# Twelve weight granules multiplied as plain float32, and fewer weight subtractions on GpSimd, in a chain of two transformer blocks

## The chip, the cores and the metric

The kernel runs on one core of one Trainium2 chip, as one program. The metric is the time of one execution in microseconds (us) on the device; the number to be forecast is the median of the runs. All data are float32.

## What is computed

Two blocks follow each other on 256 tokens of 2048 features. `w_o`, `w_up`, `cc_in` and `cc_out` below are the weights of the four products that the change touches (`cc_in` and `cc_out` are `w_in` and `w_out` of `conformer_conv`).

```python
# first block
mod = c_act @ w_ada + b_ada                    # six vectors: sh1, sc1, gt1, sh2, sc2, gt2
h = rmsnorm(x, g_mix) * (1 + sc1) + sh1
x = x + (1 + gt1) * mixer(h, ...)              # ends with  merged @ w_o
h = rmsnorm(x, g_ffn) * (1 + sc2) + sh2
u = h @ w_up                                   # 2048 -> 11264
x = x + (1 + gt2) * ((silu(a) * b) @ w_down)   # a, b: u after three taps along tokens
x = rmsnorm(x, g_final)
# second block
h = rmsnorm_2(x, norm1_g)
# conformer_conv(h, ...):
u = h @ w_in + b_in                            # cc_in, 2048 -> 4096
u = val * sigmoid(gate)
u = causal_dwconv(u, dw) + dw_b                # 31 taps along tokens
u = silu(layernorm(u, ln_g, ln_b))
x = x + u @ w_out + b_out                      # cc_out, 2048 -> 2048
x = x + square(relu(rmsnorm_2(x, norm2_g) @ w1)) @ w2
x = rmsnorm_2(x, final_g)
```

## The kernel before

**Granules.** Every weight matrix is cut into granules of 128 x 1024 floats (512 KB). SyncE issues their transfers in the order of use (`issue`, L191) into a ring of six buffers named `raw`. TensorE multiplies float32r numbers, which keep less of a float than float32; so each granule is split into two parts: ScalarE copies it to float32r (`hi`, `split_hi`, L196, four buffers), and VectorE or GpSimd subtracts that copy from the raw granule (`lo`, `split_lo`, L204, three buffers). The operand is split the same way, two feature tiles at a time, into a tile `xs` (eight buffers). TensorE then sums three products per tile (`products`, L252): hi with the operand's hi, hi with its lo, lo with its hi. A granule is two row tiles of four output tiles, so it makes 2 x 4 x 3 = 24 matmuls of 128 x 256. Eight granules fill a group of four output tiles over all 2048 input features; the products here consist of such groups (`gemm`, L277), four for `w_o` and `cc_out`, 22 for `w_up`, seven for `cc_in` and two of half the width for `cc_last`, which is the rest of the same matrix.

**Order.** The program is written as a list of items, one a granule, and emitted item by item; each engine works through its own instructions in that order. When item i's matmuls are emitted, `hi` is emitted up to item i + 3, and operand preparation and `lo` up to item i + 2 (`split_to`, LA = 2). A raw buffer is free again when its `lo` is done, two granules ahead of the matmuls. Some items carry a granule of `w_ada` as an extra: a dot product on VectorE (L374), placed by `fill_ada`; the first 74 units of the last three tiles of the modulation (`IN_MIX`) lie among the items of `w_in`, the remaining 22 among those of `w_o`.

**Which engine subtracts.** The table `GPSIMD` names the granules whose `lo` GpSimd makes: `w_o` 0 to 7, `w_up` 10 to 17, `cc_in` from 8 on and `cc_last`, `cc_out` 0 to 7 (and every third granule of another stretch). VectorE makes all others.

**Operands at the four places.** In the first group of `w_o` the operand pairs come from the merged gates `mg`, which VectorE is still finishing (L868, L875, L876), by `o_prep`: a copy on ScalarE (L226) and a subtraction on VectorE (L227). The first groups of `w_up` and `cc_in` take x without the norm's factor r, which isn't known yet (`early_up`, `early_prep`, through `split_scaled`, L273 and L274); their sums are scaled afterwards. r is computed while granule 4 of that group is emitted (`norm2`, `norm3`). The second groups take the normed operand: `h_prep` for `w_up` (VectorE L581, ScalarE L582, VectorE L588) and `g_prep` for `cc_in` (VectorE L603, ScalarE L604, VectorE L608), pair by pair. In `cc_in` VectorE also runs the 31 taps, with the running sum in PSUM (L1178, L1181). `cc_out` waits behind a barrier (`ln`): the layer norm's mean and factor come from TensorE (L390), then `s_first` subtracts the mean and multiplies by the factor on VectorE into one of two pair tiles (L1349, L1350), ScalarE applies silu (L1353) and copies (L1354), and `s_second` subtracts (L1358); `rescale` of x (L1118) lies between.

Of the kernel before, what the change touches and what calls it, by code (L numbers as in the profile page):

```python
# [18 lines left out]
P = 128  # L19
# [18 lines left out]
# columns of the packed per-feature vectors, in the two parts they are loaded in  # L38
# [20 lines left out]
# columns of the constants  # L59
# [33 lines left out]
class Item:  # L93
    """One granule of matrix products: half a unit of weights, and what goes with it."""

    def __init__(self, uses, mm=None):
        self.uses, self.mm = uses, mm
        self.pool = False
        self.prep = self.post = self.barrier = self.also = self.enter = None
        self.extra = []  # L100
# [3 lines left out]
def block_kernel(ctx: ExitStack, tc: tile.TileContext, t):  # L104
# [3 lines left out]
    GPSIMD = {"w_up": (10, 18), "w_o": (0, 8), "cc_in": (8, 54), "cc_last": (0, 8), "cc_out": (0, 8)}  # L108
    SIDE = 4
    P13, S14, P14, S15, P15 = 8, 10, 12, 8, 14  # L110
    IN_MIX = 74
# [36 lines left out]
    def second_vectors():  # L148
        """What the feed-forwards need takes the place of the activated condition."""
# [28 lines left out]
    items = []  # L178
    epi = deque()
# [18 lines left out]
    def split_lo(it):  # L198
        it.lo = wp.tile([P, 1024], FR, tag="lo", name="lo")
        w, k = it.uses  # L200
        # VectorE is busy with the operands of a first group, and with the convolution
# [5 lines left out]
    class Pairs:  # L207
        """Operands as pairs of feature tiles, each split into two float32r parts."""
# [15 lines left out]
    def split_x(dst, src):  # L224
        """dst: [P, 2, 2, S] float32r; src: [P, 2, S]."""
        nc.scalar.activation(dst[:, 0], src, AF.Copy)  # L226
        nc.vector.tensor_tensor(dst[:, 1], src, dst[:, 0].bitcast(F32), op=OP.subtract)  # L227

    def products(it, ps, xs, k0, kpg, nk, G, tok):
        """The products of one granule; the operand of the first row tile starts the sums."""  # L230
# [23 lines left out]

    def outputs(ps, G, tok, cols=S):
# [4 lines left out]
    def finish_epis(seq):  # L260
        """The epilogues of groups up to that number."""
# [7 lines left out]
    def split_scaled(dst, p, scale):  # L269
        """A pair of tiles of x, each times its column."""  # L270
# [6 lines left out]
    def gemm(w, g, nk, xs, epis, G=4, prep=None, tok=False, barrier=None, post=None, hook=None,  # L277
             whole=False):
        """One group of G output tiles: nk row tiles of the weights in granules of 1024 columns."""
# [5 lines left out]
        def mm(it, k0):  # L285
# [5 lines left out]
            products(it, st["ps"], xs, k0, kpg, nk, G, tok)  # L291
# [8 lines left out]
        for gi in range(ng):  # L300
            it = Item((w, g * ng + gi), lambda it, k0=gi * kpg: mm(it, k0))
            if prep:
                it.prep = lambda k0=gi * kpg: prep(k0 // 2)
# [6 lines left out]
    def lead(w, sets, chunks, xs, prep, feed):  # L310
        """Sets of four groups that take turns in all banks, by chunks of pairs of row tiles; between
        its turns a group's sums wait where its results will go."""
# [55 lines left out]
    def ada(n, half):  # L368
        """Half of the products of one tile of the modulation."""
# [8 lines left out]
    def ada_sum(a, b):  # L378
        """The modulation's tiles a to b of six."""
# [5 lines left out]

    def spread(cols, name):
        """[tokens, 2] to [P, S], the same in every partition."""
# [14 lines left out]
    class Stat:  # L402
        """Sums of squares over the features of tiles that come one by one, and with a gain those
        of the scaled features too: the early tiles' are added up first, the late ones go straight
        to the tensor engine, as [tokens, block * count + which]."""
# [51 lines left out]
    def rope(dst, ps, which, then=None):  # L457
        """dst = ps * cos + swapped halves * signed sin."""
# [13 lines left out]

    def start():
# [20 lines left out]
        # the first norm's sums, between the products of the first rows' modulation  # L494
# [29 lines left out]
    def angles():  # L524
        """The angles of both tables, reduced to -pi..pi."""
# [13 lines left out]
    def tables(w):  # L539
        """Cosine and signed sine from the reduced angle."""  # L540
# [9 lines left out]
    def piped(first, second, n):  # L550
        """A step of preparation that starts the next pair before it ends its own."""
# [16 lines left out]
    def h_prep(A, B, ready=None):  # L568
        """Pairs of (x * rstd) * A + B."""
# [22 lines left out]
    def g_prep(A):  # L592
        """Pairs of x * A * rstd."""
# [1044 lines left out]
```

## Time and profile before

| what | value |
|---|---|
| runs, us | 2649.13, 2643.74, 2645.97 (median 2645.97) |
| profiled execution, span from first to last instruction | 2641.8 us |
| profiled execution, time of its own as a run | not stated; its span is 1.9 us below the fastest run and 4.2 us below the median |
| mean granted TensorE clock | 0.993 |
| TensorE busy | 2568.7 us, 97% of the span |
| VectorE busy | 1884.2 us, 71% |
| ScalarE busy | 1414.5 us, 54% |
| GpSimd busy | 306.8 us, 12% |
| `hi` on ScalarE | 858 granules, mean 1061 ns |
| `lo` on VectorE | 771 granules, mean 1229 ns |
| `lo` on GpSimd | 87 granules, mean 2485 ns |

A profile lists, for each engine, groups of instructions by source line with the idle time just before them and the instruction that ended it. An engine that is idle and is not the one that sets the end costs nothing. The granted clock is the share of TensorE's full speed: 1.00 is its upper level of 2.4 GHz, 0.50 its lower level of 1.2 GHz. One matmul of two float32r tiles is one row of the trace; one of plain float32 is two.

### The profile page before, as it was taken

To read this page: it belongs to the slowest core of one execution; us is meant where nothing else is said; L and a number is where in the kernel's file an instruction comes from. 1 tells how busy PE (TensorE), PEld (TensorE's weight loads), DVE (VectorE), ACT (ScalarE), POOL (GpSimd) and SP (SyncE) were. 2 spreads that over 40 slices of the span, in tenths; PEclk is the share of its full clock that TensorE was granted. 3 is DMA by queue.
4 is the path that set the end of the run, shared out by engine and by line. 5 is a ranking of instruction groups with operands and counts; after the bars stand their busy time and mean duration, and the time that the engine had idled before them with its cause. 6 is when DMAs were issued, how large, how long until landed. Compare 5 with 4: busy or idle time off the path is not lost.

```text
span 2641.8 us, 51155 instructions
## 1 busy us (share of the span) xinstructions
PE 2568.7 (97%) x20774; PEld 2520.1 (95%) x20774; DVE 1884.2 (71%) x2742; ACT 1414.5 (54%) x2039; POOL 306.8 (12%) x206
## 2 busy tenths in 40 slices
PE   6999999999899999999999998998999999999998
PEld 5899999999898999999999998998999999999998
DVE  6887877868879666677677679987644444666765
ACT  5776664445346444444565555655544444555553
POOL 1201200000303000000000018983000000000000
PEclk9999999999999999999999999999999999999999
DMA  9998767778784777676555554434555555555553
GB/s 320 321 333 316 246 222 240 252 242 281 242 298 162 229 225 223 224 224 224 190 184 185 185 180 143 163 128 141 174 188 184 184 186 186 180 184 185 186 184 125
DMA packets 153599, 559.35 MB, mean 212 GB/s; under 512 B 17041, under 2 KB 17425, under 8 KB 153361
## 3 DMA queue, kind: packets, MB, share of 16 engines
q1 hardware_dynamic: 153362, 556.08, 62.9%
q8 instruction: 162, 2.65, 0.4%
q14 instruction: 75, 0.61, 0.1%
HBM read 553.91 MB, written 2.10 MB: 210 GB/s over the span
## 4 chain that ended last, share of the span: by engine, by line
PE 56%; issue 32%; DVE 8%; DMA 1%; ACT 1%; POOL 1%; DVEq 0%; POOLq 0%; SPq 0%; ACTq 0%
PE g L252 50%; PE v L252 3%; DVE lo L204 1%; DVE raw L374 1%; DMA raw<-in_w_ada 1%; DVE dc L1181 1%; PE ln L1225 0%; DVE xs L608 0%; DVE vec L603 0%; DMA raw<-in_w_in 0%; DVE hn L581 0%; POOL side L1168 0%; DVE xs L588 0%; DVE xs L227 0%; DVE xs L1358 0%
## 5 line engine op out<-in xcount | busy, mean ns | idle before, releaser
L252 PE MATMUL g<-xs,hi 128*128 128x256 f32 x12640 | 2283.0, 283 | 26.7 <-DVE xs L588 6.4
L252 PEld LDWEIGHTS g<-xs,hi 128*128 128x128 f32 x12640 | 1957.7, 190 | 36.6 <-DVE xs L608 7.3
L252 PE MATMUL g<-xs,lo 128*128 128x256 f32 x6320 | 1785.6, 283 | 5.1 <-DVE lo L204 5.1
L196 ACT ACTIVATE hi<-raw 128x1024 fp32r<-128x1024 f32 x858 | 910.1, 1061 | 1029.5 <-PE g L252 590.9
L204 DVE TENSOR_TENSOR lo<-raw,hi 128x1024 fp32r<-128x1024 f32 x771 | 946.8, 1229 | 436.1 <-PE g L252 237.6
L252 PEld LDWEIGHTS g<-xs,lo 128*128 128x128 f32 x6320 | 1200.3, 190 | 6.2 <-DVE lo L204 6.1
L204 POOL TENSOR_TENSOR lo<-raw,hi 128x1024 fp32r<-128x1024 f32 x87 | 215.8, 2485 | 558.6 <-PE g L252 417.0
L374 DVE SCALAR_TENSOR_TENSOR raw<-raw,crow 128x1024 f32<-128x1024 f32 x192 | 242.8, 1267 | 13.9 <-DMA raw<-in_w_ada 13.4
L227 DVE TENSOR_TENSOR xs<-hid,xs 128x512 fp32r<-128x512 f32 x128 | 88.7, 693 | 120.0 <-ACT xs L226 119.7
L1181 DVE SCALAR_TENSOR_TENSOR dc<-gu,vec,dc 128x256 f32<-128x256 f32 x372 | 148.6, 483 | 0.2
L227 DVE TENSOR_TENSOR xs<-f,xs 128x512 fp32r<-128x512 f32 x88 | 61.0, 693 | 76.1 <-ACT xs L226 75.9
L399 POOL TENSOR_TENSOR small<-small,mh 128x2 f32<-128x2 f32 x3 | 2.9, 979 | 927.7 <-DVE small L398 927.7
L252 PE MATMUL v<-xs,hi 128*128 128x256 f32 x512 | 92.0, 281 | 0.0
L1083 POOL TENSOR_TENSOR small<-small,mh 128x2 f32<-128x2 f32 x1 | 0.7, 693 | 722.2 <-DVE small L1084 722.2
L252 PEld LDWEIGHTS v<-xs,hi 128*128 128x128 f32 x512 | 79.0, 189 | 0.0
L226 ACT ACTIVATE xs<-hid 128x512 fp32r<-128x512 f32 x128 | 78.6, 615 | 0.0
L252 PE MATMUL v<-xs,lo 128*128 128x256 f32 x256 | 72.5, 283 | 1.3 <-DVE lo L204 1.3
L226 ACT ACTIVATE xs<-f 128x512 fp32r<-128x512 f32 x88 | 54.1, 615 | 0.0
L252 PE MATMUL g<-hi,xs 128*128 128x512 f32 x128 | 43.3, 410 | 9.3 <-ACT xs L582 6.8
L252 PEld LDWEIGHTS v<-xs,lo 128*128 128x128 f32 x256 | 48.4, 189 | 1.6 <-DVE lo L204 1.5
L991 ACT ACTIVATE cv<-g,vec 128x256 f32<-128x256 f32 x84 | 45.9, 546 | 0.0
L1168 POOL TENSOR_TENSOR side<-side,tap 128x256 f32<-128x256 f32 x58 | 44.9, 786 | 3.0 <-ACT tap L1165 1.9
(270 smaller groups left out, 1376.9 us busy)
## 6 DMA issues: line engine op xcount, KB each, us to landing
raw<-in_w SPq DMA_DIRECT2D x256, 512.0 KB, 3.4
raw<-in_w_ada SPq DMA_DIRECT2D x192, 512.0 KB, 4.8
raw<-in_w_in SPq DMA_DIRECT2D x176, 512.0 KB, 4.7
raw<-in_w_up SPq DMA_DIRECT2D x176, 512.0 KB, 4.2
raw<-in_w_down SPq DMA_DIRECT2D x88, 512.0 KB, 3.3
raw<-in_cc_in SPq DMA_DIRECT2D x56, 512.0 KB, 3.3
raw<-in_w_o SPq DMA_DIRECT2D x32, 512.0 KB, 4.8
raw<-in_cc_out SPq DMA_DIRECT2D x32, 512.0 KB, 3.3
```

Source lines behind the costliest of these rows:

```text
L196: nc.scalar.activation(it.hi, raws[it.uses], AF.Copy)
L204: eng.tensor_tensor(it.lo, raws[it.uses], it.hi.bitcast(F32), op=OP.subtract)
L226: nc.scalar.activation(dst[:, 0], src, AF.Copy)
L227: nc.vector.tensor_tensor(dst[:, 1], src, dst[:, 0].bitcast(F32), op=OP.subtract)
L252: nc.tensor.matmul(o, l, r, start=(first and n == 0), stop=(last and n == 2), skip_group_check=True)
L374: nc.vector.scalar_tensor_tensor(r, r, 1.0, two["c"][:, half * 1024:(half + 1) * 1024], op0=OP.mult, op1=OP.mult, accum_out=part[:, half, ...
L399: nc.gpsimd.tensor_tensor(v, v, mh, op=OP.pow)
L991: nc.scalar.activation(u, ps, AF.Identity, scale=w[2], bias=vcol("conv_b", j))
L1083: nc.gpsimd.tensor_tensor(r2, r2, mh, op=OP.pow)
L1168: nc.gpsimd.tensor_tensor(sums, sums, x, op=OP.add)
L1181: return lambda: nc.vector.scalar_tensor_tensor(acc["t"], u[:, k:k + S], w(k), acc["t"], op0=OP.mult, op1=OP.add)
```

## The change

The first three granules of the first group of `w_o`, `w_up`, `cc_in` and `cc_out` become plain: 8 float32 matmuls on the raw weights and the unsplit operand, with no `hi`, no `lo` and no `xs`. Their raw buffers are free only when TensorE has read them. The unsplit operand is `mg`, x scaled on ScalarE into a free place (`xv`), and `cu`. `w_o` and `cc_out` need the split pairs 0 to 2 from their second group on: these are made during that group. In the second groups of `w_up` and `cc_in` pair 0 is prepared right after r, and the others earlier than before by up to two granules (`ahead`). GpSimd keeps the `lo` of `cc_in` and `cc_last` alone; 24 others leave it, six of which belong to plain granules, so 18 go to VectorE. In `cc_out` the normed operand is made in place, so the preparation no longer waits for one of two pair tiles. `rescale` starts four items later. Four more granules of `w_ada` move into `w_in`, and none lies in the first four items of `w_o`. The diff also drops comments and docstrings, so line numbers shift (before to after): L204 to L216, L227 to L239, L374 to L403, L581 to L610, L588 to L617, L868 to L897, L1349 to L1400, L1350 to L1401, L1358 to L1411. The plain matmuls are at L275.

```diff
-    GPSIMD = {"w_up": (10, 18), "w_o": (0, 8), "cc_in": (8, 54), "cc_last": (0, 8), "cc_out": (0, 8)}
+    GPSIMD = {"cc_in": (8, 54), "cc_last": (0, 8)}
+    PO, PU, PC, PL = 3, 3, 3, 3
-    IN_MIX = 74
+    IN_MIX = 78
+    def also(n, f):
+        g = items[n].also
+        items[n].also = (lambda: (g(), f())) if g else f
+    def ahead(prep):
+        return lambda p: [prep(q) for q in ((1, 2) if p == 0 else (p + 2,)) if q < KD // 2]
+    def plain_products(it, ps, x, cols, k0, kpg, nk, G):
+        outs = outputs(ps, G, False, cols)
+        w = raws[it.uses]
+        for kk in range(kpg):
+            k = k0 + kk
+            for i in range(G):
+                c = (kk * G + i) * P
+                nc.tensor.matmul(outs[i], w[:, c:c + P], x(k), start=(k == 0 and (i % 2 == 0 or len(ps) == G)),
+                                 stop=(k == nk - 1), skip_group_check=True)
...
-            products(it, st["ps"], xs, k0, kpg, nk, G, tok)
+            if it.plain:
+                plain_products(it, st["ps"], plain, xs.cols, k0, kpg, nk, G)
+                used(it.uses)
+            else:
+                products(it, st["ps"], xs, k0, kpg, nk, G, tok)
...
+            it.plain = plain is not None and gi < {"w_o": PO, "w_up": PU, "cc_in": PC, "cc_out": PL}[w]
...
-    def o_prep(p):
-        split_x(xs_o.new(p), m[f"mg{p // 4}"][:, 2 * (p % 4):2 * (p % 4) + 2])
+    def o_prep(p, late=False):
+        if (p < PO) == late:
+            split_x(xs_o.new(p), m[f"mg{p // 4}"][:, 2 * (p % 4):2 * (p % 4) + 2])
...
-             prep=o_prep if i == 0 else None, hook=o_start if i == 0 else None)
+             prep=(o_prep, lambda p: o_prep(p, True))[i] if i < 2 else None, hook=o_start if i == 0 else None,
+             plain=(lambda k: m[f"mg{k // 8}"][:, k % 8]) if i == 0 else None)
...
-    fill_ada(us[IN_MIX:], n1, len(items) - 4)
+    fill_ada(us[IN_MIX:], n1 + 4, len(items) - 4)
...
+        if p < PU:
+            if p == 0:
+                m["xv"] = slot(7, "xv").rearrange("p a s -> p (a s)")[:, 0:2 * PU * (S + 2)].rearrange(
+                    "p (k s) -> p k s", s=S + 2)
+            for k in (2 * p, 2 * p + 1):
+                nc.scalar.activation(m["xv"][:, k, 0:S], xres[:, k], AF.Copy, scale=aff[:, 2, k:k + 1])
...
+            return
         split_scaled(xs_v.new(p), p, lambda k: aff[:, 2, k:k + 1])
...
-        gemm("w_up", g, KD, xs_u if g else xs_v, es, prep=(early_up, prep_u)[g] if g < 2 else None)
+        gemm("w_up", g, KD, xs_u if g else xs_v, es, prep=(early_up, ahead(prep_u))[g] if g < 2 else None,
+             plain=None if g else lambda k: m["xv"][:, k])
     items[n2 + 4].also = norm2
+    also(n2 + 5, lambda: prep_u(0))
...
+        if p < PC:
+            if p == 0:
+                m["xv"] = slot(6, "xv")
+            for k in (2 * p, 2 * p + 1):
+                nc.scalar.activation(m["xv"][:, k], xres[:, k], AF.Copy, scale=aff[:, 4, k:k + 1])
+            return
         split_scaled(xs_0.new(p), p, lambda k: aff[:, 4, k:k + 1])
...
-             prep=(early_prep, prep_c)[g] if g < 2 else None)
+             prep=(early_prep, ahead(prep_c))[g] if g < 2 else None, plain=None if g else lambda k: m["xv"][:, k])
     items[at_cc + 4].also = norm3
+    also(at_cc + 5, lambda: prep_c(0))
...
+        bg.extend([lambda: None] * 4)
         for j in range(KD):
             bg.append(lambda j=j: rescale(j))
...
     def s_first(p):
-        d = xs_s.new(p)
-        us[p] = u = pair_tile()
-        c = m["u"][p // 4][:, 2 * (p % 4):2 * (p % 4) + 2]
-        nc.vector.tensor_tensor(u, c, wide(stage["mu"]), op=OP.subtract)
+        u = normed(p)
+        nc.vector.tensor_tensor(u, u, wide(stage["mu"]), op=OP.subtract)
         nc.vector.tensor_tensor(u, u, wide(stage["r1"]), op=OP.mult)
...
-        nc.scalar.activation(d[:, 0], u, AF.Copy)
+        if p >= PL:
+            nc.scalar.activation(xs_s.new(p)[:, 0], u, AF.Copy)
...
+    def s_late(p):
+        if p < PL:
+            split_x(xs_s.new(p), normed(p))
...
-             prep=s_prep if i == 0 else None, barrier=ln if i == 0 else None)
+             prep=(s_prep, s_late)[i] if i < 2 else None, barrier=ln if i == 0 else None,
+             plain=(lambda k: m["u"][k // 8][:, k % 8]) if i == 0 else None)
...
-            if items[x].uses:
+            if items[x].uses and not items[x].plain:
                 split_lo(items[x])
...
-                if items[at["hi"]].uses:
+                if items[at["hi"]].uses and not items[at["hi"]].plain:
                     split_hi(items[at["hi"]])
```

Three places where the order of VectorE's instructions is different (rows are line, operation, out<-in, size, and how many in sequence):

VectorE where `w_o` begins; before, `xs<-mg` are the pairs 0 to 2, and the `lo` of their granules are GpSimd's:

```order
L868 TENSOR_TENSOR mg_7374<-g,ga_5122 128x256
L374 SCALAR_TENSOR_TENSOR raw,part<-raw,crow 128x1024
L227 TENSOR_TENSOR xs<-mg_6819,xs 128x2x256
L868 TENSOR_TENSOR mg_7374<-g,ga_5122 128x256
L374 SCALAR_TENSOR_TENSOR raw,part<-raw,crow 128x1024
L227 TENSOR_TENSOR xs<-mg_6819,xs 128x2x256
L868 TENSOR_TENSOR mg_7374<-g,ga_5122 128x256
L374 SCALAR_TENSOR_TENSOR raw,part<-raw,crow 128x1024
L227 TENSOR_TENSOR xs<-mg_6819,xs 128x2x256
```

and in the changed kernel, where the first `xs` is that of pair 3 and a `lo` follows it:

```order
L897 TENSOR_TENSOR mg_7386<-g,ga_5128 128x256
L216 TENSOR_TENSOR lo<-raw,hi 128x1024
L897 TENSOR_TENSOR mg_7386<-g,ga_5128 128x256 x3
L410 TENSOR_TENSOR mod<-part 128x16
L411 TENSOR_TENSOR mod<-mod,vec 128x16
L989 TENSOR_SCALAR aff<-mod 128x16
L904 TENSOR_TENSOR mb<-g,gb_6414 128x256
L239 TENSOR_TENSOR xs<-mg_6831,xs 128x2x256
L216 TENSOR_TENSOR lo<-raw,hi 128x1024
```

Three operand splits and three dot products of `w_ada` are gone from between and behind the last `mg` products; the subtractions of granules 3 to 7 of the group are now on VectorE, one behind each `xs`.

VectorE from the moment when r of `w_up` is there (`hn` is the normed x, `xs<-hn` the operand's lo, `vec<-g` the scaling of the first group's sums); before:

```order
L204 TENSOR_TENSOR lo<-raw,hi 128x1024
L581 SCALAR_TENSOR_TENSOR hn<-xres,aff,r_9141 128x256 x2
L588 SCALAR_TENSOR_TENSOR xs<-hn,mod,xs 128x256 x2
L581 SCALAR_TENSOR_TENSOR hn<-xres,aff,r_9141 128x256 x2
L204 TENSOR_TENSOR lo<-raw,hi 128x1024
L581 SCALAR_TENSOR_TENSOR hn<-xres,aff,r_9141 128x256 x2
L588 SCALAR_TENSOR_TENSOR xs<-hn,mod,xs 128x256 x2
L204 TENSOR_TENSOR lo<-raw,hi 128x1024
L581 SCALAR_TENSOR_TENSOR hn<-xres,aff,r_9141 128x256 x2
L588 SCALAR_TENSOR_TENSOR xs<-hn,mod,xs 128x256 x2
L1037 TENSOR_TENSOR vec_8771<-g,r_9141 128x256
```

and in the changed kernel:

```order
L216 TENSOR_TENSOR lo<-raw,hi 128x1024
L610 SCALAR_TENSOR_TENSOR hn<-xres,aff,r_9010 128x256 x2
L617 SCALAR_TENSOR_TENSOR xs<-hn,mod,xs 128x256 x2
L610 SCALAR_TENSOR_TENSOR hn<-xres,aff,r_9010 128x256 x4
L617 SCALAR_TENSOR_TENSOR xs<-hn,mod,xs 128x256 x2
L610 SCALAR_TENSOR_TENSOR hn<-xres,aff,r_9010 128x256 x2
L617 SCALAR_TENSOR_TENSOR xs<-hn,mod,xs 128x256 x2
L216 TENSOR_TENSOR lo<-raw,hi 128x1024
L610 SCALAR_TENSOR_TENSOR hn<-xres,aff,r_9010 128x256 x2
L617 SCALAR_TENSOR_TENSOR xs<-hn,mod,xs 128x256 x2
L216 TENSOR_TENSOR lo<-raw,hi 128x1024
L610 SCALAR_TENSOR_TENSOR hn<-xres,aff,r_9010 128x256 x2
```

Before, the two `lo` between the first scalings belong to granules 6 and 7 of the first group, and those of the second group are GpSimd's; now `lo` of granule 0 of the second group stands behind three operand pairs, and one `lo` behind each further pair.

VectorE where `cc_out` begins; before:

```order
L1349 TENSOR_TENSOR vec_8771<-cu,mu 128x512
L1350 TENSOR_TENSOR vec_8771<-vec_8771,rb 128x512
L1358 TENSOR_TENSOR xs<-vec_8771,xs 128x2x256
L1349 TENSOR_TENSOR vec_8771<-cu,mu 128x512
L1350 TENSOR_TENSOR vec_8771<-vec_8771,rb 128x512
L1349 TENSOR_TENSOR vec_8771<-cu,mu 128x512
L1350 TENSOR_TENSOR vec_8771<-vec_8771,rb 128x512
L1358 TENSOR_TENSOR xs<-vec_8771,xs 128x2x256
```

and in the changed kernel:

```order
L1400 TENSOR_TENSOR cu<-cu,mu 128x512
L1401 TENSOR_TENSOR cu<-cu,rb 128x512
L1400 TENSOR_TENSOR cu<-cu,mu 128x512
L1401 TENSOR_TENSOR cu<-cu,rb 128x512
L1400 TENSOR_TENSOR cu<-cu,mu 128x512
L1401 TENSOR_TENSOR cu<-cu,rb 128x512
L1400 TENSOR_TENSOR cu<-cu,mu 128x512
L1401 TENSOR_TENSOR cu<-cu,rb 128x512
L1400 TENSOR_TENSOR cu<-cu,mu 128x512
L1401 TENSOR_TENSOR cu<-cu,rb 128x512
L1411 TENSOR_TENSOR xs<-cu,xs 128x2x256
L216 TENSOR_TENSOR lo<-raw,hi 128x1024
```

Five pairs are normed ahead of the first operand split, which is now that of pair 3, with its granule's `lo` behind it.

## Rows read from the trace of the kernel before

**Rows 1.** The page's head and its part 1, TensorE: busy us, share, instructions.

```profile
span 2641.8 us, 51155 instructions
PE 2568.7 (97%) x20774; PEld 2520.1 (95%) x20774; DVE 1884.2 (71%) x2742; ACT 1414.5 (54%) x2039; POOL 306.8 (12%) x206
```

**Rows 2.** Waits of TensorE, whole span: line waited for, us in total, times, longest.

```profile
PE g L252 <- DVE xs L588: 6.4, 4, 1.8
PE g L252 <- DVE xs L608: 6.3, 5, 2.5
PE g L252 <- DVE xs L1358: 4.1, 6, 1.3
PE g L252 <- DVE xs L227: 3.5, 1, 3.5
PE g L252 <- DVE mg L868: 3.5, 1, 3.5
...
PE g L252 <- ACT xs L1354: 2.6, 1, 2.6
PE ln L1225 <- DVE cu L1185: 2.5, 1, 2.5
```

**Rows 3.** Windows of L252: stretch, its us, TensorE busy (matmuls), weight loads, clock.

```profile
684.00:724.00 40.00, 32.91 (x240) 32.50 (x239) 0.87 0.68 233
820.00:848.00 28.00, 21.57 (x162) 20.74 (x161) 0.94 0.41 146
1588.00:1616.00 28.00, 21.88 (x150) 20.93 (x149) 0.88 0.41 132
1796.00:1800.00 4.00, 2.69 (x12) 2.52 (x12) 0.50 0.64 236
860.00:880.00 20.00, 20.00 (x171) 20.00 (x170) 1.00 0.68 230
```

**Rows 4.** Timeline of TensorE ahead of `cc_out`: start, us, engine, line, count.

```profile
1784.65 4.57 PE L1212 MATMUL g<-gu,dg 128*128 128x256 f32 x20
1789.06 0.50 PE L1230 MATMUL ln<-con,cu 128*128 128x1 f32 x4
```

**Rows 5.** Timeline of VectorE at `w_o`: the same operation long and short.

```profile
689.93 2.82 DVE L227 TENSOR_TENSOR xs<-mg,xs 128x512 fp32r<-128x512 f32 x1
...
694.14 0.68 DVE L227 TENSOR_TENSOR xs<-mg,xs 128x512 fp32r<-128x512 f32 x1
```

**Rows 6.** Timeline of GpSimd at `w_o`, [idle before <-releaser].

```profile
689.12 3.08 POOL L204 TENSOR_TENSOR lo<-raw,hi 128x1024 fp32r<-128x1024 f32 x1 [0.20 <-POOL lo L204]
```

**Rows 7.** Timeline of VectorE from r of `w_up`.

```profile
812.36 0.88 DVE L581 SCALAR_TENSOR_TENSOR hn<-xres,aff,r 128x256 f32<-128x256 f32 x2 [0.24 <-ACT r L983]
813.70 0.89 DVE L588 SCALAR_TENSOR_TENSOR xs<-hn,mod,xs 128x256 fp32r<-128x256 f32 x2 [0.46 <-ACT xs L582]
...
815.30 1.22 DVE L204 TENSOR_TENSOR lo<-raw,hi 128x1024 fp32r<-128x1024 f32 x1
...
819.15 5.15 DVE L581 SCALAR_TENSOR_TENSOR hn<-xres,aff,r 128x256 f32<-128x256 f32 x2
```

**Rows 8.** Timeline of TensorE: r's sums between granules 5 and 6 of `w_up`.

```profile
811.66 0.48 PE L252 MATMUL g<-xs,hi 128*128 128x258 f32 x2
```

**Rows 9.** Timeline of VectorE in `cc_in`: the first scaling, and taps.

```profile
1577.31 2.68 DVE L603 SCALAR_TENSOR_TENSOR vec<-xres,aff,r 128x256 f32<-128x256 f32 x2 [0.26 <-ACT r L1090]
...
1613.58 11.05 DVE L1181 SCALAR_TENSOR_TENSOR dc<-gu,vec,dc 128x256 f32<-128x256 f32 x28
```

**Rows 10.** Timelines at `cc_out`: ScalarE's silu, TensorE's start, VectorE.

```profile
1793.79 1.09 ACT L1353 ACTIVATE vec<-vec 128x256 f32<-128x256 f32 x2 [1.36 <-DVE vec L1350]
...
1795.60 0.58 PE L252 MATMUL g<-xs,hi 128*128 128x256 f32 x1 [2.56 <-ACT xs L1354]
...
1826.12 1.23 DVE L204 TENSOR_TENSOR lo<-raw,hi 128x1024 fp32r<-128x1024 f32 x1 [1.21 <-PE g L252]
```

**Rows 11.** The page's part 6, DMA issues: KB each, us to landing.

```profile
raw<-in_w_o SPq DMA_DIRECT2D x32, 512.0 KB, 4.8
```

More of the change, by code (lines that the diff above doesn't have):

```diff
@@ L98, in __init__ @@
         self.pool = False
+        self.plain = False
         self.prep = self.post = self.barrier = self.also = self.enter = None
@@ L277, in gemm @@
     def gemm(w, g, nk, xs, epis, G=4, prep=None, tok=False, barrier=None, post=None, hook=None,
-             whole=False):
+             whole=False, plain=None):
         kpg = 1024 // (G * P)
@@ L1024, in early_up @@
             finish_epis(gseq[0])
+        if p < PU:
[4 more added lines that the diff above has]
+                nc.scalar.activation(m["xv"][:, k, 0:S], xres[:, k], AF.Copy, scale=aff[:, 2, k:k + 1])
+            b = mod[:, 3 * KD + 2 * p:3 * KD + 2 * p + 2].rearrange("p (a o) -> p a o", o=1).to_broadcast([P, 2, 2])
+            nc.scalar.activation(m["xv"][:, 2 * p:2 * p + 2, S:], b, AF.Copy)
+            return
         split_scaled(xs_v.new(p), p, lambda k: aff[:, 2, k:k + 1])
@@ L1341, in wide, with normed @@
         return x.rearrange("p (o s) -> p o s", o=1).to_broadcast([P, 2, S])
-    us = {}
+    def normed(p):
+        return m["u"][p // 4][:, 2 * (p % 4):2 * (p % 4) + 2]
     def s_first(p):
-        d = xs_s.new(p)
-        us[p] = u = pair_tile()
-        c = m["u"][p // 4][:, 2 * (p % 4):2 * (p % 4) + 2]
-        nc.vector.tensor_tensor(u, c, wide(stage["mu"]), op=OP.subtract)
+        u = normed(p)
+        nc.vector.tensor_tensor(u, u, wide(stage["mu"]), op=OP.subtract)
         nc.vector.tensor_tensor(u, u, wide(stage["r1"]), op=OP.mult)
@@ L1353, in s_first @@
             nc.scalar.activation(u[:, i], u[:, i], AF.Silu, scale=vcol("ln_g", k), bias=vcol("ln_b", k))
-        nc.scalar.activation(d[:, 0], u, AF.Copy)
+        if p >= PL:
+            nc.scalar.activation(xs_s.new(p)[:, 0], u, AF.Copy)
     def s_second(p):
-        d = xs_s.at(p)
-        nc.vector.tensor_tensor(d[:, 1], us.pop(p), d[:, 0].bitcast(F32), op=OP.subtract)
+        if p >= PL:
+            d = xs_s.at(p)
+            nc.vector.tensor_tensor(d[:, 1], normed(p), d[:, 0].bitcast(F32), op=OP.subtract)
+    def s_late(p):
+        if p < PL:
+            split_x(xs_s.new(p), normed(p))
     s_prep = piped(s_first, s_second, KD // 2)
```

## The prediction
> **What bounds the kernel now.** I first read the page's head: the span is 2641.8 us and TensorE is busy for 97% of it [rows 1]. So the kernel can gain in two ways only: TensorE gets less work, or its few gaps close. The change gives it more work, so all hope lies in the gaps. The list of TensorE's waits says what ended them [rows 2]: at `w_o` two waits of 3.5 us, for `mg` (L868) and for the first operand splits (L227); in the second groups of `w_up` and `cc_in` 6.4 and 6.3 us for operand splits (L588, L608); at the start of `cc_out` 2.6 us for ScalarE's copy and 4.1 us for operand splits (L1358). All name VectorE or the copy ahead of it, and all lie where the change is made.
>
> Waits alone are too small a price, because TensorE's clock falls after some of them. So I counted the matmuls of L252 in windows [rows 3]. Undisturbed, 171 start in 20 us: 0.117 us each, and a split granule of 24 takes 2.81 us. What a stretch loses is its length less its matmuls at that rate. At `w_o` (684 to 724) 240 matmuls: 40 - 28.1 = 11.9 us lost, with 7.1 us of waiting and the rest, 4.8, in two falls of the clock (mean 0.87), 2.4 us each. At `w_up` (820 to 848) 28 - 19.0 = 9.0 us. At `cc_in` (1588 to 1616) 28 - 17.5 = 10.5 us. At `cc_out` the first group runs from 1795.60 to about 1826.1, where VectorE's next subtraction waited for its last granule to be used [rows 10]: 30.5 us, against 22.5 undisturbed, so 8.0 lost. In all 39 us, 1.5% of the span.
>
> Then I asked why VectorE is late. The same split of an operand pair at `w_o` takes 0.68 us in one row and 2.82 us in another [rows 5], and the long one began inside a GpSimd subtraction of 3.08 us (689.12 to 692.20) [rows 6]. At `w_up` a pair of scalings takes 0.88 us, but 5.15 us when it starts at 819.15 [rows 7]. The taps of `cc_in`, whose running sum is in PSUM, are not stretched: 28 in 11.05 us, 0.395 each [rows 9], while GpSimd subtracts. So VectorE's two-input operations from SBUF pay for GpSimd's subtractions, by some 2 us each.
>
> **What a plain granule costs.** The trace has plain float32 matmuls with 128 x 256 operands and fresh weights for each: ten of them (20 records) from 1784.65 until the next line at 1789.06 [rows 4], 0.441 us each. Eight make 3.53 us, against 2.81 split: +0.72 us a granule, +8.6 us for twelve, all of it on TensorE's path. The Trainium skill speaks more strongly against the change: its page "FP8 and Floating Point Precision", in "TensorE Precision Notes", has a true float32 product pass four times through the array, which at the split form's rate here is 32 passes against 24, by estimate 3.74 us a granule; the sum below would be 2.6 us smaller by it (2631.5 us). The rows of this kernel, two records of a matmul and not four, give the smaller price, and I use that.
>
> **The sum, place by place.**
>
> `w_o`. Gone from VectorE in the 32 us around the start are the stretching of its rows (eight GpSimd subtractions, some 14 us by the difference of long and short rows), three splits of 0.68 us and some dot products of `w_ada`; new are five subtractions of 1.22 us [rows 7], 6.1 us. VectorE gains by far, and the first three granules wait for no split at all, only for `mg`. Of the 11.9 us I take 1.0 as left (short waits where granules 3 to 7 meet the last `mg`), and 2.2 go to the plain granules: gain 8.7. Bounds: 9.7 with no wait left; 5.2 if one wait of 3.5 us stays.
>
> `w_up`. r is ready at 812.36 [rows 7], and the second group could start when granules 6 and 7 are through, 5.6 us after 811.66 [rows 8], at 817.3, so 4.9 us after r. The changed order puts ahead of the first `lo` of that group four pairs of scalings and three of splits, which follow each other at 0.80 us, the wait of 0.5 for ScalarE's first copy, and then 1.22 for itself: 5.6 + 0.5 + 1.2 = 7.3 us after r. TensorE waits 2.2 us (its first two matmuls need no `lo`). Per granule after that VectorE has two pairs of operations and a `lo`, 0.8 + 0.8 + 1.13 = 2.73 us, with 0.33 to 0.5 more where the first group's sums are scaled, against TensorE's 2.81: a lag of 0.9 over the group. Left are 3.1 us of the 9.0, plain granules take 2.2: gain 3.7. Bounds: 4.6 without the lag; 0 if the clock falls after the first wait (2.4) and the lag is 1.3 more. The delay of plain granules moves r too, so the 4.9 us stay.
>
> `cc_in`. GpSimd keeps its subtractions, so the stretching stays (the first scaling after r takes 2.68 us [rows 9]). The eight operand pairs now come ahead of the first 14 operations of the taps: 12 at 0.395 and a pair at 0.86, 5.6 us, which is what the operands can win. But VectorE works without a pause from r until long after these groups, and TensorE later waits 2.5 us for the finished taps [rows 2]: what is taken from the first waits is asked for there. Bounds: -2.2 (plain granules alone) and 5.6 - 2.2 = +3.4. I take the middle, 0.6.
>
> `cc_out`. The first matmul needs silu alone, which ends at 1793.79 + 1.09 = 1794.9 [rows 10], not the copy or the split. The clock is at its lower level then (0.50 from 1796 to 1800, where 12 matmuls took 2.69 us, 0.224 each [rows 3], 1.9 times the usual). If it rises at 1800 again, six plain matmuls are done by then at 0.84 us, 18 more take 7.9 us, and five split granules 14.05: the group ends at 1822.0 instead of 1826.1. VectorE's five normed pairs end by 1800 and each further pair with its `lo` costs 3.3 us, so the last `lo` is there at about 1815, before its use: no wait. Gain 4.1. Bounds: 6.6 with a clock that is never low, 2.2 if it stays low for 4 us more.
>
> The other edits I cost at nothing, and name their cover: 18 `lo` of 1.22 us on VectorE (22 us, counted above at each place) lie under TensorE with VectorE at 71%; the late pairs 0 to 2 of `w_o` and `cc_out` lie in second groups, where an operand is needed a whole group later; ScalarE loses 12 copies. The plain granules' raw buffers are free about three granules later, but a transfer that waits for one is needed five granules (14 us) after that and takes 4.8 us to land [rows 11], plus 1.06 for `hi` and 1.2 for `lo`: 7 us to spare. If that cover goes, each granule late adds its lateness in full.
>
> Sum: 8.7 + 3.7 + 0.6 + 4.1 = 17.1 us. Against the profiled execution that is a span of 2624.7; the median of the runs is 4.2 us above that span, so the forecast of the median is 2645.97 - 17.1 = **2628.9 us**. With all low ends the gain is 5.2, with all high ends 24.3: 2621.7 to 2640.8.
>
> **The rivals.** A difference under 0.2%, 5.3 us, is what a measurement of this kernel can't tell from none.
>
> 1. *Every gap closes.* All 39 us come back and only the 8.6 are paid: about 2615.5. For it: every wait at these places names VectorE. Against: the first wait at `w_up` follows from the order, and `cc_in` keeps GpSimd. 8%.
> 2. *VectorE stays the bound* at `w_up` and `cc_in`: the waits move from operand splits to `lo`, with a fall of the clock; gains 5.2, 0, -2.2 and 4.1, about 2638.9, and as far as 2643 with two falls of the clock (2.4 each) more. For it: the thin margin of 2.73 against 2.81 us. Against: the stretching is gone at `w_up`. 22%, of which 9 within 0.2%.
> 3. *The change doesn't do what it says*, that is, the rows are stretched by something other than GpSimd's subtractions: the waits at `w_o` and `w_up` remain, plain granules cost 8.6, and what is left is `cc_out` (6.3 before its plain granules' cost) and the 2.8 of `cc_in`: 0.5 us, about 2645.5. Against it stand the unstretched taps. 5%.
> 4. *Slower: the ring of raw buffers runs dry.* Three of six are held until TensorE has read them. If landing takes over 4.8 + 7 = 11.8 us when the transfers of `w_ada` lie between, TensorE stands once at each place for landing, `hi` and `lo` (7.1 us) and a fall of the clock (2.4), 9.5 us four times, 38 against the 17.1: about 2667. Against it: the share of the transfer engines there (the last number but one) is 0.41 to 0.68 [rows 3]. 5%.
>
> **How the numbers follow.** The forecast's own case has 60%, all of it faster. Faster: 60 + 8 + 13 and 1 of case 3, 0.82; within 0.2%: 9 and the other 4 of case 3, 0.13; slower 0.05. The range leaves out cases 1, 3 and 4 (18%) and holds the forecast's bounds and case 2: 2620 to 2643.
>
> **What would show it.** In the profile of the changed kernel: plain matmuls at L275 at 0.44 us (24 of them in 10.6 us at full clock); no row of L239 or L617 near 2 us at `w_o` and `w_up`; TensorE's two 3.5 us waits gone and 684 to 724 holding a clock near 1.00; one wait of about 2 us for `lo` at the start of the second group of `w_up`; `cc_in` with waits for L637 still there; `cc_out` starting on silu. The forecast is wrong if a plain matmul takes over 0.6 us, if waits for `raw` appear, or if the gains of `cc_in` and `w_up` come out of these bounds.

## The result, and the profile after

The changed kernel takes **2623.94 us** (median of four runs, 2622.43 to 2625.61); the kernel before, over the runs beside it, 2644.85. The ratio is 0.9921, 95% interval 0.9909 to 0.9933: 20.9 us faster, where 17.1 was forecast, and the time lies in the range. The profiled execution took 2623.79 us with a span of 2622.0, so 1.8 us lie outside the span.

The page's head and part 1 of the changed kernel answer to [rows 1]:

```profile
span 2622.0 us, 50874 instructions
PE 2571.0 (98%) x20678; PEld 2518.2 (96%) x20678; DVE 1849.0 (71%) x2739; ACT 1404.1 (54%) x2027; POOL 245.0 (9%) x182
```

TensorE is busy 2.3 us longer and the span is 19.8 us shorter: gaps have closed. What ends its waits now (the same view as [rows 2], first rows left out where they lie elsewhere):

```profile
PE g L264 <- DVE lo L216: 8.2, 6, 2.4
...
PE g L264 <- POOL lo L216: 5.6, 4, 2.0
...
PE g L275 <- ACT cu L1404: 1.4, 1, 1.4
```

No operand split is left among them at the four places. At `w_o` TensorE doesn't wait at all; at `w_up` one wait of 1.60 us is left, for a VectorE subtraction; the four waits for GpSimd are all in the second group of `cc_in`; and `cc_out` starts on silu. The timeline of TensorE in the changed kernel (start, us, line, count, and in brackets the idle time before) shows the three kinds of places:

```profile
689.33 10.53 PE L275 MATMUL g<-mg,raw 128*128 128x256 f32 x48
699.50 0.58 PE L264 MATMUL g<-xs,hi 128*128 128x256 f32 x2
...
809.85 0.40 PE L264 MATMUL g<-xs,hi 128*128 128x256 f32 x2
811.85 0.38 PE L264 MATMUL g<-xs,lo 128*128 128x256 f32 x1 [1.60 <-DVE lo L216]
...
1563.58 0.61 PE L419 MATMUL rb<-con,small 128*128 128x128 f32 x4
...
1774.63 0.71 PE L419 MATMUL mu<-con,small 128*128 128x128 f32 x4 [0.25 <-DVE small L1376]
1775.80 0.71 PE L419 MATMUL rb<-con,small 128*128 128x128 f32 x4 [0.46 <-POOL small L1380]
1777.92 13.38 PE L275 MATMUL g<-cu,raw 128*128 128x256 f32 x48 [1.41 <-ACT cu L1404]
1790.95 0.58 PE L264 MATMUL g<-xs,hi 128*128 128x256 f32 x2
```

The 24 plain matmuls of `w_o` are 48 records and take 699.50 - 689.33 = 10.17 us, 0.424 each.

Such rows are landmarks that every variant of this kernel has, so its time can be cut into stages: the moment when TensorE has finished `w_in` (689.60 before, 689.33 after); the first matmul of `w_up`, the first that is 258 columns wide (792.31, 782.83); the first matmul of its second group (817.46, 809.85); the spreading of r ahead of the second group of `cc_in` (1576.25, 1563.58); that of the mean ahead of `cc_out` (1791.15, 1774.63); the first operand of the product after it (VectorE, 1890.1, 1869.8); the end. Stages in us, of one profiled execution each:

| stage | before | after | gain | forecast |
|---|---|---|---|---|
| up to `w_o` | 689.60 | 689.33 | 0.3 | 0 |
| `w_o` | 102.71 | 93.50 | 9.2 | 8.7 |
| first group of `w_up` | 25.15 | 27.02 | -1.9 | in the next |
| rest of `w_up`, `w_down`, first group of `cc_in` | 758.79 | 753.73 | 5.1 | 3.7 less 2.2 of `cc_in` |
| second group of `cc_in` to its layer norm | 214.90 | 211.05 | 3.9 | 0.6 and 2.2 |
| `cc_out` | 98.95 | 95.17 | 3.8 | 4.1 |
| the rest | 751.70 | 752.20 | -0.5 | 0 |

Where two executions run the same code in a stage, it agrees within 0.2 us, with these exceptions: the one up to `w_o` varies by 3.1 us over the runs below, the last by 1.4, `cc_out` by its clock, `cc_in` once by 1.6 and `w_o` once by 1.0. The medians of the runs are therefore better for totals, and the stages for what happened where.

### The profile page after: what moved, and what is told of

It is laid out like the page before. It is cut to its first block, busy times and chain, and to the rows that moved or that the text cites. A ratio compares the mean times of both kernels' runs of the same rounds, so it can differ in the third digit from the quotient of the medians.

```text
span 2622.0 us, 50874 instructions
## 1 busy us (share of the span) xinstructions
PE 2571.0 (98%) x20678; PEld 2518.2 (96%) x20678; DVE 1849.0 (71%) x2739; ACT 1404.1 (54%) x2027; POOL 245.0 (9%) x182
## 4 chain that ended last, share of the span: by engine, by line
PE 59%; issue 33%; DVE 6%; DMA 1%; ACT 1%; POOL 0%; DVEq 0%; POOLq 0%; SPq 0%
PE g L264 52%; PE v L264 3%; DVE lo L216 2%; DVE raw L403 1%; PE g L275 1%; PE g L1255 1%; DMA raw<-in_w_ada 1%; PE ln L1268 0%; DVE vec L632 0%; DVE swp L494 0%; PE idx L711 0%; DVE score L720 0%; DVE xs L617 0%; DMA raw<-in_w_in 0%; DVE m L719 0%
## 5 line engine op out<-in xcount | busy, mean ns | idle before, releaser
L264 PE MATMUL g<-xs,hi 128*128 128x256 f32 x12472 | 2242.3, 282 | 1.6 <-ACT g L357 1.1
L264 PEld LDWEIGHTS g<-xs,hi 128*128 128x128 f32 x12472 | 1923.4, 189 | 8.0 <-issue 4.3
L264 PE MATMUL g<-xs,lo 128*128 128x256 f32 x6236 | 1757.2, 282 | 11.0 <-POOL lo L216 5.6
L208 ACT ACTIVATE hi<-raw 128x1024 fp32r<-128x1024 f32 x846 | 897.6, 1061 | 1027.5 <-PE g L264 592.5
L216 DVE TENSOR_TENSOR lo<-raw,hi 128x1024 fp32r<-128x1024 f32 x783 | 963.2, 1231 | 425.4 <-PE g L264 227.9
L264 PEld LDWEIGHTS g<-xs,lo 128*128 128x128 f32 x6236 | 1179.3, 189 | 13.3 <-POOL lo L216 6.6
L403 DVE SCALAR_TENSOR_TENSOR raw<-raw,crow 128x1024 f32<-128x1024 f32 x192 | 236.8, 1236 | 14.2 <-DMA raw<-in_w_ada 14.1
L239 DVE TENSOR_TENSOR xs<-hid,xs 128x512 fp32r<-128x512 f32 x128 | 88.7, 693 | 120.1 <-ACT xs L238 119.7
L216 POOL TENSOR_TENSOR lo<-raw,hi 128x1024 fp32r<-128x1024 f32 x63 | 156.0, 2485 | 148.8 <-DVE raw L403 79.7
L239 DVE TENSOR_TENSOR xs<-f,xs 128x512 fp32r<-128x512 f32 x88 | 61.0, 693 | 75.1 <-ACT xs L238 74.9
```

The costliest lines, as they stand in the source:

```text
L208: nc.scalar.activation(it.hi, raws[it.uses], AF.Copy)
L216: eng.tensor_tensor(it.lo, raws[it.uses], it.hi.bitcast(F32), op=OP.subtract)
L264: nc.tensor.matmul(o, l, r, start=(first and n == 0), stop=(last and n == 2), skip_group_check=True)
L403: nc.vector.scalar_tensor_tensor(r, r, 1.0, two["c"][:, half * 1024:(half + 1) * 1024], op0=OP.mult, op1=OP.mult, accum_out=part[:, half, ...
```

## The experiments

Times are medians of four runs, with their 95% interval against the kernel before; stages are named as in the table and come from one execution each. The kernel before was run again beside each batch, with medians of 2643.57, 2643.85 and 2643.33 us against the 2644.85 above; so times of two batches compare to some 1.5 us, and the gain against the kernel before is the safer number.

### The table alone

```diff
-    GPSIMD = {"w_up": (10, 18), "w_o": (0, 8), "cc_in": (8, 54), "cc_last": (0, 8), "cc_out": (0, 8)}
+    GPSIMD = {"cc_in": (8, 54), "cc_last": (0, 8)}
```

in the kernel before.

> The kernel before with the changed table alone: GpSimd subtracts for cc_in only, no plain granules, no earlier operands. Theory (GpSimd's subtractions stretch VectorE's two-input operations, and that is what made the operands late): the long rows at w_o and w_up are gone (no L227 or L588 row over 1 us there), the gain is 6 at w_o and 3 at w_up, 0 at cc_in, 0 at cc_out, in all about 9 us, 2636. Rival (the plain granules make the gain, GpSimd's share is small): 2 us or less, 2643 or more, since VectorE gets 24 subtractions of 1.22 us.

Measured: 2625.51 us, ratio 0.9927 (0.9913 to 0.9942). Nearly the whole gain, with one line changed. `w_o` takes 91.71 us, less than the 93.50 with plain granules; the long stage after the first group of `w_up` 751.80, 7.0 less than before; `cc_in` 216.39, nothing gained; `cc_out` 97.33, 1.6 less. The operand splits at `w_o` (timeline of VectorE of this run):

```profile
690.30 0.69 DVE L227 TENSOR_TENSOR xs<-mg,xs 128x512 fp32r<-128x512 f32 x1
...
693.51 0.69 DVE L227 TENSOR_TENSOR xs<-mg,xs 128x512 fp32r<-128x512 f32 x1
```

Where [rows 5] have 2.82 and 0.68 us, all eight are 0.69 now, and no L588 row at `w_up` is over 0.49. So the theory holds, and its size was twice what I expected; the rival falls.

### The table of before in the changed kernel

The reverse of that line, with all else as changed.

> The changed kernel with the table of before: GpSimd subtracts again at w_o, w_up and cc_out. Theory (stretching): waits come back at w_o (granules 3 to 7) and w_up, about 12 of the 20 us are lost, near 2636. Rival (plain granules and the order make the gain): at most 4 us lost, 2628 or less.

Measured: 2628.64 us, ratio 0.9940 (0.9925 to 0.9955), a gain of 14.9 us where the changed kernel has 20.9. That misses the theory (2636) and lies close to the rival's 2628. At `w_o` nothing is lost (93.51 against 93.50): VectorE's rows are stretched again, but with three plain granules and the dot products of `w_ada` out of the way TensorE waits for none of them. At `w_up` 5.5 us are lost (759.23 against 753.73), the earlier operands notwithstanding. At `cc_out` nothing (95.25). My theory was wrong about `w_o`: there the table is enough, and so are plain granules with the new places of `w_ada`.

### No plain granules

```diff
-    PO, PU, PC, PL = 3, 3, 3, 3
+    PO, PU, PC, PL = 0, 0, 0, 0
```

> The changed kernel with no plain granule (all four counts 0), its table, its order of operands and its in-place norm kept. Theory: a plain granule costs TensorE 0.72 us, 2.2 at each place, and pays only where the first operand is late (w_o, cc_out). So w_o loses 2 to 4 us of its gain, cc_out 1 to 2, and w_up and cc_in win up to 2 each; in all within 3 us of the changed kernel, 2621 to 2627. Rival (plain granules carry the gain at all four): 8 us or more lost, 2632 or more.

Measured: **2619.86 us**, ratio 0.9905 (0.9890 to 0.9920), 4.1 us faster than the changed kernel by the medians and 2.8 by the gains, and faster than either side had it. `w_o` takes 91.33 us (2.2 less), the first group of `w_up` 25.16 (1.9 less), the stage with the first group of `cc_in` 752.09 (1.6 less), `cc_in` the same 210.95, `cc_out` 96.09 (0.9 more). I expected `w_o` to lose without them; they are a price at three of the four places, 5.7 us together.

### Operands not earlier

The changed kernel without `ahead` and without the two early pairs:

```diff
-             prep=(early_prep, ahead(prep_c))[g] if g < 2 else None, plain=None if g else lambda k: m["xv"][:, k])
+             prep=(early_prep, prep_c)[g] if g < 2 else None, plain=None if g else lambda k: m["xv"][:, k])
...
-    also(at_cc + 5, lambda: prep_c(0))
```

and the same at `w_up`.

> The changed kernel without the earlier operands of the second groups of w_up and cc_in (pair 0 right after r, others two granules ahead): each pair is prepared when it was before. Theory: at w_up the work from r to the last operand is the same, only its order differs; the first subtraction comes earlier and the splits later, so 0 to 2 us lost there. At cc_in the taps come between the pairs again, 2 us lost. In all 1 to 4 us, 2625 to 2628. Rival (the order carries the gain at w_up and cc_in): 7 us or more lost, 2631 or more.

Measured: 2626.55 us, ratio 0.9933 (0.9917 to 0.9950), 2.6 slower than the changed kernel by the medians and 3.9 by the gains. `w_up` doesn't need the order (753.40 against 753.73). `cc_in` does: 215.12 us, as before the change. TensorE's waits there, from 1550 to 1640 in this run:

```profile
PE g L264 <- DVE xs L637: 7.9, 5, 3.1
PE ln L1268 <- DVE cu L1228: 1.0, 1, 1.0
```

So the 3.9 us of `cc_in` come from the order alone, twice what I had given it here.

### VectorE subtracts the whole second group of `cc_in`

On top of no plain granules: `GPSIMD = {"cc_in": (16, 54), "cc_last": (0, 8)}`.

> The changed kernel without plain granules, and GpSimd subtracts for cc_in from granule 16 on, not from 8: the whole second group's eight subtractions go to VectorE. Theory (VectorE's chain from r through eight operand pairs to the finished taps sets the end of this stretch): eight times 1.13 us are added, the stretching that goes with GpSimd is some 9 to 12 us, so the chain is as long as before within 3 us and the first matmul for the layer norm's sums comes at the same time within 3 us; the total is 2617 to 2623, although TensorE's waits for GpSimd's subtractions (5.4 us) are gone. Rival (those waits set the time): 5 us or more faster than without this edit, 2615 or less.

Measured: 2617.19 us, ratio 0.9897 (0.9883 to 0.9912), 2.7 less than without plain granules. Without this edit VectorE's chain from r to the last operand split ran from 1558.72 to 1585.5; with it, and with five subtractions of its own in between, it runs from 1559.37 to 1579.3. The first and the last row of it, with the first subtraction:

```profile
1559.37 0.88 DVE L632 SCALAR_TENSOR_TENSOR vec<-xres,aff,r 128x256 f32<-128x256 f32 x2 [0.27 <-ACT r L1133]
...
1565.27 1.22 DVE L216 TENSOR_TENSOR lo<-raw,hi 128x1024 fp32r<-128x1024 f32 x1
...
1578.64 0.69 DVE L637 TENSOR_TENSOR xs<-vec,xs 128x512 fp32r<-128x512 f32 x1
```

20.0 us instead of 26.8, though 5 x 1.13 = 5.7 us of work were added: the stretching had cost 12.5 us in this chain. Without the edit (the run with no plain granules), six of its 16 scalings were stretched, as GpSimd made six subtractions beside it; one place, VectorE and then GpSimd:

```profile
1578.81 5.08 DVE L632 SCALAR_TENSOR_TENSOR vec<-xres,aff,r 128x256 f32<-128x256 f32 x2
```

```profile
1578.73 4.87 POOL L216 TENSOR_TENSOR lo<-raw,hi 128x1024 fp32r<-128x1024 f32 x2 [3.85 <-PE g L264]
```

With the edit that pair takes 0.87. From r's sums to the first matmul of the layer norm's sums it is 47.0 us instead of 50.4, but TensorE waits 2.6 us for the taps there:

```profile
PE ln L1268 <- DVE cu L1228: 2.6, 1, 2.6
```

So the total fell as the theory said and not as far as the rival said, but the theory's premise was off. The chain to the taps did not stay as long: it lost more stretching (12.5 us) than the 9.0 us that eight subtractions add, and the layer norm's sums came 3.4 us earlier, a little over the 3 allowed. Behind that the taps on VectorE set the end.

### Plain granules in `cc_out` alone

`PO, PU, PC, PL = 0, 0, 0, 3`.

> The changed kernel with plain granules in cc_out alone. Theory (a plain granule pays where the first operand is late): TensorE starts 2.3 us earlier there (silu and not the copy ends its wait) and pays 1.9 us for three plain granules: within 2 us of no plain granules, 2618 to 2622. Rival (float32 is a loss everywhere, or its start under a low clock costs more): 3 us or more slower, 2623 or more.

Measured: 2619.55 us, ratio 0.9907 (0.9892 to 0.9922), the same as with none. `cc_out` takes 93.76 us; the runs with plain granules there took 93.8 to 95.3, those without but with the in-place norm 95.5 to 97.0, so that 1.6 us between the means (94.7 and 96.3) are theirs. Each start falls under the low clock, and where the clock rises differs between executions of the same code: the changed kernel's windows (us, TensorE busy and count, weight loads, VectorE, ScalarE, GpSimd, mean granted clock, share and GB/s of the transfers) still show 0.56 until 1784,

```profile
1776.00:1780.00 4.00, 2.59 (x9) 2.04 (x9) 3.45 (x7) 2.28 (x5) 0.00 (x0) 0.59 0.02 4
1780.00:1784.00 4.00, 4.00 (x11) 3.21 (x11) 3.43 (x6) 3.74 (x7) 0.00 (x0) 0.56 0.00 0
```

while this run, whose plain granules began at 1774.24, had 0.87 from 1776 to 1780 and 1.00 behind it:

```profile
1776.00:1780.00 4.00, 4.00 (x17) 3.40 (x17) 3.42 (x7) 3.52 (x6) 0.00 (x0) 0.87 0.00 0
```

In the total those 1.6 us do not show.

### The order alone

No plain granules, and the table of before.

> The changed kernel without plain granules and with the table of before: what is left is the earlier operands, the in-place norm and the places of the w_ada granules. Theory (GpSimd's stretching makes the operands late, and plain granules only hide it): the waits at w_o come back, 6 us or more of the 11.9 lost there; at w_up 5 lost; cc_in keeps 4; in all 12 us or more slower than without plain granules, 2632 or more. Rival (the order carries the gain): 2625 or less.

Measured: 2628.72 us, ratio 0.9940 (0.9924 to 0.9957), 8.9 us slower than without plain granules: between the two again, so neither held. `w_o` takes 96.71: 5.4 us more than with the new table (the theory said 6 or more), yet 6.0 less than before, where the places of the `w_ada` granules are all that differs in this stage. The stage after the first group of `w_up` loses 4.7. The rows show stretching and its cause side by side; VectorE of this run at `w_o`, and GpSimd:

```profile
694.81 2.33 DVE L989 TENSOR_SCALAR aff<-mod 128x16 f32<-128x16 f32 x1
697.06 0.41 DVE L904 TENSOR_TENSOR mb<-g,gb 128x256 f32<-128x256 f32 x1
697.40 0.68 DVE L239 TENSOR_TENSOR xs<-mg,xs 128x512 fp32r<-128x512 f32 x1
698.00 2.63 DVE L905 TENSOR_TENSOR mg<-mg,mb 128x256 f32<-128x256 f32 x1
700.54 0.41 DVE L904 TENSOR_TENSOR mb<-g,gb 128x256 f32<-128x256 f32 x1
```

```profile
694.72 2.39 POOL L216 TENSOR_TENSOR lo<-raw,hi 128x1024 fp32r<-128x1024 f32 x1 [0.79 <-PE g L264]
697.59 5.30 POOL L216 TENSOR_TENSOR lo<-raw,hi 128x1024 fp32r<-128x1024 f32 x2 [0.47 <-PE g L264]
```

The operation that started at 694.81 under a subtraction begun at 694.72 ended as that one did, at 697.1; the next stretched one, at 698.00, lies under the subtractions begun at 697.59. The L904 at 697.06 says nothing, since it ran almost wholly between two subtractions; but the one at 700.54 ran under the second of the pair, reads one operand from PSUM and takes its usual 0.41.

### The `w_ada` granules where they were

No plain granules, `IN_MIX = 74` and the rest from the first item of `w_o` on.

> The changed kernel without plain granules and with the w_ada granules where they were before (74 in w_in, the rest from the first item of w_o on). Theory: VectorE's dot products among the first operand splits of w_o are what the table alone left there, 3 us: w_up starts 2 to 3.5 us later, in all 2622 to 2624. Rival: no difference, 2618 to 2621.

Measured: 2619.36 us, ratio 0.9907 (0.9892 to 0.9922): no difference, as the rival had it. Its `w_o` takes 92.74 us, 1.4 more, but the table alone has the same instructions there and takes 91.71. The trace puts most of the 1.0 between them down to a transfer: ScalarE's `hi` at 709.03 had waited 4.28 us for a granule of `w_o`, and behind it TensorE waited 0.75 us. So with the new table their place is worth 0.4 to 1.4 us; with the old one it was 6.0 (above).

### What a plain granule costs by itself

The changed kernel with `PO = 8`: all of the first group of `w_o` plain; a single run.

> The changed kernel with all eight granules of the first group of w_o plain. No wait of TensorE is left at w_o in the changed kernel, so this measures the price of a plain granule by itself. Theory (0.6 to 0.7 us each): w_o takes five times that longer, 3.0 to 3.6 us. Rival (four passes against three, by the Trainium skill's page FP8 and Floating Point Precision, an estimate of 0.94 each): 4.7 us.

Measured: 2626.83 us; `w_o` takes 97.54 against 93.50, of which 0.5 is a new wait: (4.04 - 0.5) / 5 = 0.71 us a granule, at the theory's upper end. The plain records alone, 3.39 us a granule in the changed kernel against 2.81, would give 0.58; the rest of this difference in the stage's length I can't assign.

### What paid, put together

No plain granules but in `cc_out`, and `cc_in` on GpSimd from granule 16, then from granule 13.

> Everything that paid, nothing that cost: the changed kernel with plain granules in cc_out alone, and GpSimd's subtractions for cc_in from granule 16 on. Theory (the stages add up): w_o 91.3, first group of w_up 25.2, cc_in 209.2, cc_out about 94.7 us as in the runs before it, so 2614 to 2617, 7 to 10 us under the changed kernel. Rival (what is won at one place is taken at the next): 2618 or more.

> The same with GpSimd from granule 13 of cc_in on, so that five of the second group's subtractions are VectorE's. Theory: the last three operand pairs of that group are stretched again by about 1.7 us each, less 3.4 us of subtractions: cc_in within 1.5 us of that from granule 16 on. Rival (fewer subtractions on VectorE let the taps end earlier): 2 us or more faster in cc_in.

Measured: 2614.08 us, ratio 0.9892 (0.9877 to 0.9906), and **2611.89 us**, ratio 0.9884 (0.9867 to 0.9900). `cc_in` takes 207.58 and 206.66 us, within the 1.5 of the theory. That is no more than this stage varies, so which of the two is better stays open. With granule 13, one 0.47 us operation becomes 2.62 under a GpSimd subtraction, and TensorE's waits from 1550 to 1770 are short everywhere:

```profile
PE g L264 <- DVE lo L216: 1.4, 2, 1.3
PE g L275 <- ACT cu L1404: 1.4, 1, 1.4
PE g L264 <- POOL lo L216: 1.3, 2, 0.7
PE ln L1268 <- DVE cu L1228: 1.0, 1, 1.0
```

The version from granule 13 is 31.4 us faster than the kernel before, and 10.5 (by the gains) to 12.0 us (by the medians) faster than the changed kernel.

## Why the prediction was right, point by point

**What bounds the kernel** held: TensorE was busy 2.3 us longer and the time came from its gaps at the four places. The counting of lost time in windows gave 39 us; the best version has taken 32.0 us of span, so most of it was there.

**The stretching of VectorE's rows by GpSimd** held, and the table alone, which takes it away at three places, gives 18.1 us where the whole change gives 20.9. It isn't the only way: the order alone, with the old table, gives 15.1 us, and both without plain granules 23.7, so that some 9 us of it can be had by either. I had taken some 2 us a subtraction; the chain of `cc_in` shows 12.5 us for six. The Trainium skill's page "SBUF — State Buffer", section "Who interferes with whom", states this rule: an operation of VectorE with two inputs from SBUF contends with a GpSimd operation that reads SBUF, over a port pair that it calls an exclusive lock. The rows above agree: L905, with two inputs from SBUF, took 2.63 us under a GpSimd subtraction, and 0.42 in the changed kernel.

**`w_o`** (8.7 forecast, 9.2 measured): the size is right, the step behind it is not. That "the first three granules wait for no split at all" is true, but they needn't: with no plain granule `w_o` is 2.2 us shorter still. Three remedies overlap there (of 102.71 us before): the table alone gives 11.0, the places of `w_ada` alone 6.0, and plain granules with those places 9.2, so 3.2 on top under the old table and -2.2 under the new; plain granules by themselves were not run. I priced the bundle and did not ask what each part gives alone. That 8.7 came out is in part luck, since one part alone gives more.

**The price of a plain granule** (0.72 forecast) is 0.71 measured at `w_o`, and 0.6 for the three granules each of `w_up` and `cc_in`. The Trainium skill's page "FP8 and Floating Point Precision", section "TensorE Precision Notes", has four passes, which gave an estimate of 0.94. The records are two for a matmul and the time is 0.424 us, 3.6 times the 0.117 of a float32r matmul, so the measurement decides for the smaller one.

**`w_up`** (3.7 forecast): 6.7 us came back (758.79 to 752.09, where no granule is plain), 1.9 were paid for plain granules, 4.8 in all. That is 0.2 above the upper bound, no more than a stage varies. The first wait was 1.6 us and not 2.2: the first subtraction of the group was done 7.0 us after r and not 7.3, and the group was ready 5.1 us after it and not 4.9. The lag of 0.9 over the group didn't come. The last of the forecast's edits there, the earlier operands, gives nothing with the table changed.

**`cc_in`** (0.6 forecast, 2.2 measured after the price of its plain granules): here the step failed, though the bounds held. I took their middle because "what is taken from the first waits is asked for" by the taps, as if VectorE's work up to them had a fixed length. It hasn't: with operands first, the stage is 3.9 us shorter, and TensorE's wait of 2.5 us for the taps [rows 2] is gone too. VectorE's groups from r's sums to the layer norm's first matmul (`--lines`; count, then busy us and mean ns) show why. Before, from 1576.25 to 1630.6:

```profile
L1181 DVE SCALAR_TENSOR_TENSOR dc<-gu,vec,dc 128x256 f32<-128x256 f32 x52 | 20.8, 478 | 0.0
L603 DVE SCALAR_TENSOR_TENSOR vec<-xres,aff,r 128x256 f32<-128x256 f32 x16 | 15.7, 1023 | 0.3 <-ACT r L1090 0.3
L608 DVE TENSOR_TENSOR xs<-vec,xs 128x512 fp32r<-128x512 f32 x8 | 13.1, 1634 | 0.8 <-ACT xs L604 0.7
```

After, from 1563.6 to 1613.95:

```profile
L1224 DVE SCALAR_TENSOR_TENSOR dc<-gu,vec,dc 128x256 f32<-128x256 f32 x52 | 20.6, 476 | 0.0
L632 DVE SCALAR_TENSOR_TENSOR vec<-xres,aff,r 128x256 f32<-128x256 f32 x16 | 19.2, 1244 | 0.4 <-ACT r L1133 0.3
L637 DVE TENSOR_TENSOR xs<-vec,xs 128x512 fp32r<-128x512 f32 x8 | 5.5, 682 | 0.7 <-ACT xs L633 0.7
```

The taps take the same. The scalings and splits of the same operands take 28.8 us before and 24.7 after: 4.1 us less stretching, since the chain from r to the last split now meets six GpSimd subtractions and not nine. With operands first, the taps set the end only when GpSimd's share is cut as well, by 1.0 to 2.6 us.

**`cc_out`** (4.1 forecast, 3.8 measured): the plain granules took 1790.95 - 1777.92 = 13.0 us, as worked out for six under the low clock and 18 after it. That the clock rose just there is luck: over the seven executions with plain granules here the same 24 matmuls took 11.7 to 13.2 us. Some 1.6 us of the gain are theirs by the runs. The table alone gives 1.6 here, the in-place norm and the later `rescale` with the old table 3.5, and beside the in-place norm and plain granules the table gives nothing (95.25 against 95.17); how the gain divides, the clock's scatter leaves open.

The rivals: every gap closing did not happen in this kernel, though the best version passes that case's time (2615.5) by 3.6 us. VectorE as the bound came half true: TensorE's waits in `cc_in` did move from operand splits to subtractions, GpSimd's and not VectorE's, yet the stage gained, and at `w_up` one wait is left. The change doing nothing is out. The dry ring is out as a cost: no wait of TensorE names `raw` at the four places, but at `w_o` ScalarE's `hi` waits 18.7 us for transfers, before 2.3; without plain granules it is 18.6, so they are not the reason. Of the signs named in the forecast one was wrong: no wait of `cc_in` names L637 any more.

## What to carry to other kernels

When GpSimd shares elementwise work with VectorE, price what its operation does to VectorE's two-input operations beside it, not only its own time: here each subtraction moved to GpSimd took 1.13 us off VectorE and could hold it up for 2 us or more, so moving it back let VectorE finish its operands earlier. How much it is held up depends on the order of its work too: what stands beside the other engine's operation can be arranged. Before a dearer form of work is accepted as a way around a late operand, take away the reason why the operand is late; here one line gave 18.1 us, and with it changed three of four places with the dearer form only paid for it. A bundle of edits that answers one wait in several ways should be cut into its parts, since their gains overlap and their prices add.

## What the runs showed that I had not expected

An operation with a single tensor input, 128 x 16 elements, was held up too: L989 took 2.33 us under a GpSimd subtraction, and 0.18 in the changed kernel. And a median can hide what a stage shows: `w_o` took 91.29 to 91.33 us in five executions of the same code, while the stretch up to `w_o` varied from 688.82 to 691.47 in them.
